# Moving the start addresses of matmul operands apart in an fp32 encoder layer

## The chip, the cores and the metric

The kernel runs on one core of a Trainium2 chip. The metric is the device time of one execution in microseconds (us). A core has TensorE (PE: matmuls, which read SBUF and write PSUM), VectorE (DVE), ScalarE (ACT), GpSimd (POOL) and SyncE (SP), which here issues the DMAs. SBUF has 128 partitions; a tile with 128 rows lies at one byte offset in all of them, and in this document an address is that offset.

## The reference

One layer of an encoder trunk over 256 rows of 2048 channels, all in fp32. With h = RMSNorm(x):

```python
proj = h @ w_in                                  # 2048 x 18464
yr = silu(rg) * groupnorm(retention(rope(rq), rope(rk), rv))
yg = silu(gz) * rmsnorm(gated_delta(l2(silu(conv(gq))), l2(silu(conv(gk))), silu(conv(gv)), g, beta))
x = x + (sigmoid(gate_a) * yr + sigmoid(gate_b) * yg) @ w_out
x = x + cross_attention(rms_norm(x), rms_norm(mem), w_xq, w_xkv) @ w_xo     # 4 heads, 256 memory rows
x = x + square(relu(rms_norm(x) @ w_ff1)) @ w_ff2                           # hidden 8192
return rms_norm(x)
```

Nearly all of the arithmetic is the product of 256 rows with weight matrices, some 390 MB of them, each read once.

## The kernel before, in words

**Splitting.** A matmul here takes its operands in the type float32r. So that the result has fp32 precision, each operand is split in two, hi (a copy in float32r, made by ScalarE) and lo (the remainder, made by VectorE), and a product is hi x hi + hi x lo + lo x hi, three passes.

**Weights.** `fetch` loads a block of 128 x 2048 elements into a tile `raw` (three buffers) on SyncE's queue. For each half of it, L89 writes `whi` (ScalarE) and L90 writes `wlo` (VectorE), tiles of 128 x 1024 with three buffers each.

**Activations.** They lie in *quads* (`new_quad`, name `q`): one tile of 128 x 4 x 512, that is, four feature blocks, each with 256 columns of hi and 256 of lo. Three pools hold quads: five shared ones (`quad_a`: the normalised input h1, the merged mixer output, the attention output, the MLP's hidden activations), four for the memory rows in the first stage (`memq`), and four of the tail (`quad_b`: the inputs of w_xq and of the MLP's first product).

**The two matmul loops.**
- `chunk` computes 256 rows x 512 columns of a product. The stationary operand is a 128 x 128 slice of a quad, the moving one 512 columns of whi or wlo (L130: hi x hi, L131: hi x lo, L132: lo x hi): 96 matmuls a call. There are 40 calls: 4 for the values of the attention (first stage, on `memq`), 4 for the retention's v, 16 for gates, 16 for the second MLP product. The last call holds the weights of its second half in buffers of `quad_b`, where they are the moving operand.
- `blocks` computes the transpose, 256 columns as two blocks of 128. The stationary operand is a 128 x 128 slice of whi or wlo, the moving one a row of a quad: L168 takes whi against hi and lo side by side (512 columns), L169 wlo against hi (256 columns). A call has 32 such pairs, and there are 96 calls with two blocks and one with one block (L481, 16 pairs): 24 for the delta rule, 8 for the retention's q and k, 8 for the attention's keys (on `memq`), 8 for w_out, 8 for w_xq, 8 for w_xo, 32 for the first MLP product. At its end L173 (ScalarE) and L174 (VectorE) add the two halves of the sum into a tile `bo` (two buffers of 128 x 256, shared by all calls), from which the caller goes on.

**The delta rule's norms.** In `gdn_stream`, for each of eight pairs of heads, three `blocks` calls give q, k and v; then L557 and L559 compute Gram matrices in PSUM, and four instructions on L563 multiply their diagonal blocks by the identity and add up the rows, which gives the squared norms. The products themselves go to a tile `dj` that nobody reads.

**Order.** The instructions of each engine are ordered by a scheduler that simulates a timeline from the program's order, priorities and the waits between instructions and buffers. Weight loads and splits have the highest priority, evacuations of PSUM the next. `blocks` and `chunk` write two PSUM banks a call, of which there are two sets.

**Where the tiles lie.** Tiles lie one behind another in the order of the pools, each rounded up to 32 bytes. raw has 8192 bytes a partition, whi and wlo 4096, a quad 8192, all multiples of 512. So raw, whi, wlo and the five shared quads, which follow each other, start at the same remainder modulo 512. Behind them come small tiles: a scratch row of 2048 bytes, two pairs of 32, two bo of 1024, four of 32. Adding up, the tail, and with it the quads of `quad_b`, start at 192 (modulo 512, counted from raw). The constants of the mixers (768 + 32 + 512 + 1024 + 1024 + 512 + 384 + 128 bytes) come where the tail later lies, and then `memq`, at 192 + 288 = 480, that is -32.

| tiles | start modulo 512, from raw | moving and stationary operand in a matmul lie apart by |
|---|---|---|
| whi, wlo (three each), five shared quads | 0 | 0 |
| `memq` | -32 | 32 |
| `quad_b` | 192 | 192 |

The slices that a matmul takes start at multiples of 512 bytes within their tile, so the distances hold for all of them.

Of the kernel before, what the change touches and what calls it, by code (L numbers as in the profile page):

```python
# [10 lines left out]
F32 = mybir.dt.float32  # L11
F32R = mybir.dt.float32r
# [5 lines left out]
P = 128  # L18
D = 2048
S = 256  # L20
# [8 lines left out]
C_GQ, C_GK, C_GV = 6144, 8192, 10240  # L29
C_GA, C_GZ, C_TA, C_TB = 12288, 12320, 14368, 16416  # L30
THETA = 10000.0
TWO_PI = 2.0 * math.pi
BIG = 1.0e30


def _short(v, bits):
    m, e = math.frexp(v)
    return math.ldexp(math.floor(m * (1 << bits)), e - bits)


PI_1 = _short(TWO_PI, 12)
PI_2 = _short(TWO_PI - PI_1, 11)
PI_3 = float(np.float32(TWO_PI - PI_1 - PI_2))
MAGIC = 1.5 * 2.0**23
# [3 lines left out]
def trunk(ctx: ExitStack, tc: tile.TileContext, x, mem, positions, norm_mix_g, w_in, conv_w, gdn_a_log, gdn_dt_bias,  # L48
# [7 lines left out]
    wp = ctx.enter_context(tc.tile_pool(name="wpipe", bufs=3))  # L56
    hqp = ctx.enter_context(tc.tile_pool(name="hq", bufs=1))
    sm = ctx.enter_context(tc.tile_pool(name="small", bufs=2))
# [8 lines left out]
    def bank():  # L67
        return psp.tile([P, 512], F32, name="b", tag="b", bufs=4)


    def fetch(pieces, k, n, rush=False, hold=None):

        raw = wp.tile([P, k * n], F32, name="raw", tag="raw", bufs=3)
        rv = raw.rearrange("p (k n) -> p k n", k=k)
        with tc.high_priority(offset=100000):
            for off, ap in pieces:
                src = ap.rearrange("(k p) n -> p k n", p=P)
                for ks in ((slice(0, k // 2), slice(k // 2, k)) if rush else (slice(0, k),)):
                    nc.sync.dma_start(rv[:, ks, off:off + ap.shape[1]], src[:, ks, :])
            got = []  # L80
            for i in range(2):
                if hold:
                    both = hold().both
                    hi, lo = (both[:, a:a + 2, :].rearrange("p a s -> p (a s)") for a in (0, 2))
                else:
                    hi = wp.tile([P, k * n // 2], F32R, name="whi", tag="whi", bufs=3)
                    lo = wp.tile([P, k * n // 2], F32R, name="wlo", tag="wlo", bufs=3)
                src = raw[:, i * k * n // 2:(i + 1) * k * n // 2]
                act.activation(hi, src, AF.Copy)  # L89
                vec.tensor_sub(lo, src, hi.bitcast(F32))  # L90
                got.append((hi.rearrange("p (k n) -> p k n", n=n), lo.rearrange("p (k n) -> p k n", n=n)))
        return got
# [12 lines left out]
        pass  # L105

    def new_quad(pl, bufs):
        both = pl.tile([P, 4, 2 * S], F32R, name="q", tag="q", bufs=bufs)
        quad = Quad((both[:, :, 0:S], both[:, :, S:2 * S]))
        quad.both = both  # L110
        return quad

    def quad_a():
        return new_quad(hqp, 5)

    def chunk(quads, pieces_of, evac, before=None, hold=None):
# [4 lines left out]
        if hold:  # L121
            parts[1:] = [(1, 0, 256, ps[1][:, :256]), (1, 256, 512, bank()[:, :256])]
        held = {q: fetch(pieces_of(q), 4, 512, hold=hold) for q in ((2, 3) if hold else ())}

        def products(q, i, part, halves):
# [8 lines left out]
        for q in range(4):  # L134
            if q not in held:
                if before:
                    before(q)
                halves = fetch(pieces_of(q), 4, 512, rush=before is not None and q == 0)
                for i in range(4):
                    for part in parts:  # L140
                        products(q, i, part, halves)
# [10 lines left out]
    def blocks(quads, w, c0, nb, evac):  # L152

        k = 16 // nb
        ps = stream_ps()
        n = nb * P
        for g in range(KT // k):
            halves = fetch([(0, w[g * k * P:(g + 1) * k * P, c0:c0 + n])], k, n)  # L160
            for i in range(k):
                kk = g * k + i
                xh, xhl = quads[kk // 4][0][:, kk % 4, :], quads[kk // 4].both[:, kk % 4, :]
                wh, wl = halves[i // (k // 2)]
                for b in range(nb):
                    bs = slice(b * P, (b + 1) * P)
                    lh, ll = wh[:, i % (k // 2), bs], wl[:, i % (k // 2), bs]
                    pe.matmul(ps[b], lh, xhl, start=kk == 0, stop=False)  # L168
                    pe.matmul(ps[b][:, :S], ll, xh, start=False, stop=kk == KT - 1)  # L169
        for b in range(nb):  # L170
            with tc.high_priority(offset=50000):
                o = sm.tile([P, S], F32, name="bo", tag="bo", bufs=2)
                act.activation(o, ps[b][:, S:], AF.Copy)  # L173
                vec.tensor_add(o, o, ps[b][:, :S])  # L174
                evac(b, o)
# [93 lines left out]
    kt_d = dram.tile([P, KT, S], F32, name="kt_d", tag="kt_d", bufs=1)  # L269
    vv_d = dram.tile([P, NT, D], F32, name="vv_d", tag="vv_d", bufs=1)  # L270
    memq = [new_quad(kv, 4) for _ in range(4)]
    ssqm = cp.tile([P, NT, 4], F32, name="ssqm")

# [32 lines left out]
    for k2 in range(8):  # L306
# [10 lines left out]
        for f in range(2):  # L317
            k = 2 * k2 + f
# [42 lines left out]
    def rounded(o, i, scale):  # L361
        vec.tensor_scalar(o, i, scale, MAGIC, op0=ALU.mult, op1=ALU.add)
        vec.tensor_scalar(o, o, -MAGIC, None, op0=ALU.add)

    def less(k, c):
        vec.scalar_tensor_tensor(av, k, -c, av, op0=ALU.mult, op1=ALU.add)

    rounded(hv, av, 1.0 / (4096.0 * TWO_PI))
    less(hv, 4096.0 * PI_1)
    vec.scalar_tensor_tensor(lv, hv, -4096.0 * PI_2, av, op0=ALU.mult, op1=ALU.add)  # L370
    rounded(lv, lv, 1.0 / TWO_PI)
    less(lv, PI_1)
# [131 lines left out]
    mx = mixer.enter_context(tc.tile_pool(name="mix", bufs=2))  # L504
# [14 lines left out]
    def gdn_stream(grp):  # L519
# [5 lines left out]
        for pr in range(2):  # L525
# [16 lines left out]
            for b in range(2):  # L542
                kh = mx.tile([P, 2, S], F32R, name="kh", tag="kh", bufs=2)
                kl = mx.tile([P, 2, S], F32R, name="kl", tag="kl", bufs=2)
                sq = mx.tile([P, S], F32, name="sq", tag="acc", bufs=2)
                act.activation(kh, kq[:, b], AF.Copy)
                vec.tensor_sub(kl, kq[:, b], kh.bitcast(F32))
                act.activation(sq, kq[:, b, 1], AF.Square)
                g0, g1 = bank(), bank()
                g0v = g0.rearrange("p (a n) -> p a n", a=2)  # L550
                g1v = g1[:, 0:256].rearrange("p (a n) -> p a n", a=2)
                if b == 0:
                    ssq = g1[:, 256:260].rearrange("p (b i) -> p b i", b=2)
                for t in range(NT):
                    pe.matmul(ssq[:, b, t:t + 1], sq[:, t * P:(t + 1) * P], ones[:, :1], start=True, stop=True)
                for n, (l, r) in enumerate(((kh, kh), (kh, kl), (kl, kh))):
                    pe.matmul(g0v, l[:, 0, 0:P], r, start=n == 0, stop=n == 2)  # L557
                for n, (l, r) in enumerate(((kh, kh), (kh, kl), (kl, kh))):
                    pe.matmul(g1v, l[:, 0, P:S], r[:, :, P:S], start=n == 0, stop=n == 2)  # L559
                grams.append((g0v, g1v))  # L560
                for t, src in enumerate((g0v[:, 0, 0:P], g1v[:, 0, :])):
                    dj = mx.tile([P, P], F32, name="dj", tag="dj", bufs=1)
                    vec.scalar_tensor_tensor(dj, src, 1.0, ident, op0=ALU.mult, op1=ALU.mult,  # L563
                                             accum_out=ssk[:, b, t:t + 1])
            ske = mx.tile([P, 2, NT], F32, name="ske", tag="ske", bufs=2)
# [214 lines left out]
    for j in range(5):  # L780
        if j < 4:
            group = gdn_stream(j)
        if prev is not None:
            if j < 4:
                quad = mx.tile([P, 4, S], F32, name="mg", tag="mg", bufs=3)
                kept.append(quad)
            else:
                quad = quad_a()
            gates(j - 1, prev[0], prev[1], quad, take_back if j == 4 else None)
        if j < 4:  # L790
            yr = mx.tile([P, NT, 512], F32, name="yr", tag="yr", bufs=1)
            yg = mx.tile([P, NT, 512], F32, name="yg", tag="yg", bufs=1)
            retention(j, yr)
            gdn_core(j, *group, yg)
            prev = (yr, yg)
# [9 lines left out]
    def quad_b():  # L805
        return new_quad(q2p, 4)
# [181 lines left out]
def _inv_freq():  # L988
    e = np.arange(0, RDK, 2, dtype=np.float32) / np.float32(RDK)
    return (np.float32(1.0) / np.power(np.float32(THETA), e)).astype(np.float32)  # L990

# [17 lines left out]
```

## Time and profile before

| | us |
|---|---|
| median of three runs (lowest, highest) | 2132.39 (2132.25, 2138.91) |
| the profiled execution | 2133.46 |
| its span, from the first to the last instruction | 2131.7 |
| TensorE busy | 2102.5 |
| VectorE busy | 1411.9 |
| ScalarE busy | 1092.3 |

In a row of instruction groups stand the line, the engine, the operation, output and inputs by the program's names, shapes and count, then busy time in us and the mean time of one in ns, then the idle time of the engine just before them and what ended it. Matmuls overlap each other in TensorE, so the mean of one is its latency; how fast they follow each other is seen from the starts in a timeline, or from a count in a stretch of time. PEld is TensorE's load of a stationary operand, which runs beside a matmul. PEclk is the clock that TensorE was granted, in tenths.

### The profile page before, as it was taken

The numbers are of one execution on the slowest core, as the hardware profiler recorded it, in microseconds if no ns is written. First come the engines' busy times: TensorE is split into PE (matmuls) and PEld (weight loads), VectorE is DVE, ScalarE is ACT, GpSimd is POOL, SyncE is SP. The second block draws the span as 40 slices with busy tenths as digits, with TensorE's granted clock in tenths as the row PEclk, the third lists the DMA queues.
The fourth block names the chain that finished last, engine by engine and source line by source line (L and its number), as shares of the span: only waits on it lengthen the run. The fifth ranks groups of instructions, "written<-read, shape, count | busy, mean of one in ns | idle before, by whom it ended". The sixth has DMA issues, their size and how long they took to land.

```text
span 2131.7 us, 28768 instructions
## 1 busy us (share of the span) xinstructions
PE 2102.5 (99%) x11172; PEld 1798.5 (84%) x11172; DVE 1411.9 (66%) x2225; ACT 1092.3 (51%) x1700; POOL 30.6 (1%) x39
## 2 busy tenths in 40 slices
PE   8999999899999999999999999999999999999998
PEld 6878888788888888888888888888888888888887
DVE  6756779588678866786567666666556545655655
ACT  7565565364555445645456555554434434434444
POOL 0000000000000000000000000000000000000000
PEclk9999999999999999999999999999999999999999
DMA  8777665455545654565457654566556556556653
GB/s 296 248 235 250 198 194 184 131 172 190 177 148 198 198 187 135 180 203 181 157 178 251 204 180 157 176 188 189 193 189 191 184 193 194 180 197 191 185 197 139
DMA packets 316009, 405.91 MB, mean 190 GB/s; under 512 B 16592, under 2 KB 224480, under 8 KB 315744
## 3 DMA queue, kind: packets, MB, share of 16 engines
q1 hardware_dynamic: 315872, 404.08, 58.6%
q8 instruction: 87, 1.43, 0.3%
q14 instruction: 50, 0.41, 0.1%
HBM read 390.40 MB, written 13.65 MB: 190 GB/s over the span
## 4 chain that ended last, share of the span: by engine, by line
PE 94%; DMA 2%; ACT 1%; DVE 1%; issue 0%; POOL 0%; SPq 0%; ACTq 0%; POOLq 0%; DVEq 0%
PE s L168 32%; PE s L169 16%; PE s L131 13%; PE s L130 13%; PE s L132 13%; PE b L646 2%; DMA dec_d<-dec_w 1%; ACT dec_w L471 1%; PE b L557 1%; PE b L100 0%; ACT whi L89 0%; DVE wlo L90 0%; PE b L102 0%; PE b L101 0%; PE b L215 0%
## 5 line engine op out<-in xcount | busy, mean ns | idle before, releaser
L90 DVE TENSOR_TENSOR wlo<-raw,whi 128x1024 fp32r<-128x1024 f32 x702 | 858.1, 1223 | 523.5 <-ACT whi L89 518.3
L89 ACT ACTIVATE whi<-raw 128x1024 fp32r<-128x1024 f32 x702 | 742.8, 1059 | 724.2 <-PE s L132 370.2
L168 PE MATMUL s<-q,whi 128*128 128x512 f32 x3088 | 1080.1, 397 | 0.3 <-DVE q L898 0.3
L169 PE MATMUL s<-q,wlo 128*128 128x256 f32 x3088 | 845.4, 281 | 6.4 <-DVE wlo L90 6.4
L168 PEld LDWEIGHTS s<-q,whi 128*128 128x128 f32 x3088 | 571.4, 188 | 125.2 <-DVE q L898 0.5
L169 PEld LDWEIGHTS s<-q,wlo 128*128 128x128 f32 x3088 | 580.1, 188 | 21.9 <-DVE wlo L90 10.2
L131 PE MATMUL s<-wlo,q 128*128 128x512 f32 x1264 | 495.3, 392 | 0.2 <-DVE wlo L90 0.2
L132 PE MATMUL s<-whi,q 128*128 128x512 f32 x1264 | 492.0, 390 | 0.0
L130 PE MATMUL s<-whi,q 128*128 128x512 f32 x1264 | 450.1, 391 | 0.0
L131 PEld LDWEIGHTS s<-wlo,q 128*128 128x128 f32 x1264 | 237.9, 188 | 49.8 <-DVE wlo L90 1.2
L130 PEld LDWEIGHTS s<-whi,q 128*128 128x128 f32 x1264 | 237.6, 188 | 50.1 <-ACT q L228 0.4
L132 PEld LDWEIGHTS s<-whi,q 128*128 128x128 f32 x1264 | 237.6, 188 | 48.8
L173 ACT ACTIVATE bo<-s 128x256 f32<-128x256 f32 x193 | 73.1, 379 | 121.6 <-PE s L169 121.6
L174 DVE TENSOR_TENSOR bo<-bo,s 128x256 f32<-128x256 f32 x193 | 80.4, 417 | 54.0 <-ACT bo L173 53.7
L512 DVE SCALAR_TENSOR_TENSOR acc<-bo,cw,acc 128x255 f32<-128x255 f32 (+2 forms) x144 | 67.1, 477 | 4.7 <-ACT acc L509 3.3
L612 DVE TENSOR_TENSOR pr<-lw,tw 32x31 f32<-32x31 f32 (+15 forms) x124 | 40.5, 326 | 9.1 <-DMA lw<-scr_l 6.9
L614 DVE TENSOR_TENSOR tw<-tw,pr 32x31 f32<-32x31 f32 (+15 forms) x124 | 40.7, 328 | 2.4
L747 ACT ACTIVATE gth<-s 128x512 f32<-128x512 f32 x32 | 18.9, 592 | 23.1 <-PE s L132 17.5
L937 DVE SCALAR_TENSOR_TENSOR res<-s,rstd3q,res 128x512 f32<-128x512 f32 (+1 forms) x32 | 22.3, 735 | 12.0 <-PE s L132 12.0
L509 ACT ACTIVATE acc<-bo,cw 128x256 f32<-128x256 f32 x48 | 24.2, 504 | 7.3 <-DVE bo L174 5.1
L926 DVE SCALAR_TENSOR_TENSOR hs<-bo 128x256 f32<-128x256 f32 x64 | 27.0, 422 | 1.1
L929 DVE TENSOR_TENSOR q<-hs,q 128x256 fp32r<-128x256 f32 x64 | 26.8, 418 | 0.9 <-ACT q L928 0.9
(292 smaller groups left out, 1086.7 us busy)
## 6 DMA issues: line engine op xcount, KB each, us to landing
raw<-w_in SPq DMA_DIRECT2D x144, 1024.0 KB
raw<-w_ff SPq DMA_DIRECT2D x128, 1024.0 KB
raw<-w_xkv SPq DMA_DIRECT2D x31, 1024.0 KB
raw<-w_out SPq DMA_DIRECT2D x16, 1024.0 KB
raw<-w_xq SPq DMA_DIRECT2D x16, 1024.0 KB
raw<-w_xo SPq DMA_DIRECT2D x16, 1024.0 KB
dec_d<-dec_w SPq DMA_DIRECT2D x16, 192.0 KB
dec<-dec_d SPq DMA_DIRECT2D x8, 384.0 KB
```

Of the source, the lines that this page charges most:

```text
L89: act.activation(hi, src, AF.Copy)
L90: vec.tensor_sub(lo, src, hi.bitcast(F32))
L130: pe.matmul(o, xh, wh, start=first, stop=False)
L131: pe.matmul(o, xh, wl, start=False, stop=False)
L132: pe.matmul(o, xl, wh, start=False, stop=last)
L168: pe.matmul(ps[b], lh, xhl, start=kk == 0, stop=False)
L169: pe.matmul(ps[b][:, :S], ll, xh, start=False, stop=kk == KT - 1)
L173: act.activation(o, ps[b][:, S:], AF.Copy)
L174: vec.tensor_add(o, o, ps[b][:, :S])
L512: vec.scalar_tensor_tensor(acc[:, d:], ps[:, :S - d], cw[:, j, blk:blk + 1], acc[:, d:], op0=ALU.mult, op1=ALU.add)
L614: vec.tensor_sub(tw[:, j + 1:32, 0:j + 1], tw[:, j + 1:32, 0:j + 1], pv)
L646: pe.matmul(pv[:, i, :], lhs(i), rhs[:, i, :], start=True, stop=True)
```

## The change

Each tile of a quad gets 8 more elements at its end (32 bytes), and each whi and wlo 40 more (160 bytes). Nothing is read or written there; the extra elements only move what lies behind them. The tile `dj` (512 bytes) is given up: L563 now writes the first half of a tile from the two buffers of `bo`. The instructions and their sizes are the same.

```diff
+STAGGER_Q, STAGGER_W = 8, 40
...
-                    hi = wp.tile([P, k * n // 2], F32R, name="whi", tag="whi", bufs=3)
-                    lo = wp.tile([P, k * n // 2], F32R, name="wlo", tag="wlo", bufs=3)
+                    hi, lo = (wp.tile([P, k * n // 2 + STAGGER_W], F32R, name=nm, tag=nm, bufs=3)[:, :k * n // 2]
+                              for nm in ("whi", "wlo"))
...
     def new_quad(pl, bufs):
-        both = pl.tile([P, 4, 2 * S], F32R, name="q", tag="q", bufs=bufs)
+        both = pl.tile([P, 8 * S + STAGGER_Q], F32R, name="q", tag="q", bufs=bufs)
+        both = both[:, :8 * S].rearrange("p (f s) -> p f s", f=4)
...
                 for t, src in enumerate((g0v[:, 0, 0:P], g1v[:, 0, :])):
-                    dj = mx.tile([P, P], F32, name="dj", tag="dj", bufs=1)
+                    dj = sm.tile([P, S], F32, name="dj", tag="bo", bufs=2)[:, :P]
                     vec.scalar_tensor_tensor(dj, src, 1.0, ident, op0=ALU.mult, op1=ALU.mult,
                                              accum_out=ssk[:, b, t:t + 1])
```

By the same sums, the starts modulo 512 counted from raw become: whi 0, 160, 320; wlo -32, 128, 288; the shared quads -64, -32, 0, 32, 64; `memq` 64, 96, 128, 160; `quad_b` 288, 320, 352, 384. Buffers are used in rotation, so over a call a moving operand meets stationary operands at many distances.

## The prediction

> **What bounds the kernel now.** I read the page first, from the busy shares down to the costliest groups.
>
> ```profile
> span 2131.7 us, 28768 instructions
> PE 2102.5 (99%) x11172; PEld 1798.5 (84%) x11172; DVE 1411.9 (66%) x2225; ACT 1092.3 (51%) x1700; POOL 30.6 (1%) x39
> ...
> PEclk9999999999999999999999999999999999999999
> ...
> PE 94%; DMA 2%; ACT 1%; DVE 1%; issue 0%; POOL 0%; SPq 0%; ACTq 0%; POOLq 0%; DVEq 0%
> ...
> L168 PE MATMUL s<-q,whi 128*128 128x512 f32 x3088 | 1080.1, 397 | 0.3 <-DVE q L898 0.3
> L169 PE MATMUL s<-q,wlo 128*128 128x256 f32 x3088 | 845.4, 281 | 6.4 <-DVE wlo L90 6.4
> ...
> L131 PE MATMUL s<-wlo,q 128*128 128x512 f32 x1264 | 495.3, 392 | 0.2 <-DVE wlo L90 0.2
> ...
> L132 PE MATMUL s<-whi,q 128*128 128x512 f32 x1264 | 492.0, 390 | 0.0
> L130 PE MATMUL s<-whi,q 128*128 128x512 f32 x1264 | 450.1, 391 | 0.0
> ```
>
> TensorE is busy for 99% of the span, at full granted clock, and 94% of the chain of waits is TensorE. The view of waits, for TensorE alone, says how little it waits; its longest row is
>
> ```profile
> PE s L169 <- DVE wlo L90: 6.4, 8, 1.5
> ```
>
> So the time is a count of matmuls times the spacing between their starts. The 390 ns in the group rows is the latency of one, not the spacing, since they overlap. Almost everything is two loops: `chunk` (L130 to L132, 3 x 1264 = 3792 matmuls of 512 columns; moving operand whi or wlo, stationary operand a slice of a quad q) and `blocks` (3088 pairs L168 + L169; moving operand q, stationary whi or wlo). Whatever the change does must show in those spacings, and a nanosecond on each of the 3792 is 3.8 us. So I looked for stretches in which the same instruction runs with operands at different addresses. First the view of windows: stretch, its length, busy time and count of each engine, clock, DMA share, GB/s.
>
> ```profile
> core 0: us, PE busy (x) PEld busy (x) DVE busy (x) ACT busy (x) POOL busy (x), PEclk, DMA share, GB/s
> 30.00:50.00 20.00, 20.00 (x87) 15.82 (x86) 12.29 (x23) 15.36 (x26) 0.00 (x0) 1.00 0.86 303
> 1120.00:1200.00 80.00, 80.00 (x460) 69.74 (x460) 58.95 (x91) 46.88 (x75) 0.00 (x0) 1.00 0.76 237
> 1505.00:1585.00 80.00, 80.00 (x354) 66.25 (x353) 41.79 (x40) 31.68 (x33) 0.00 (x0) 1.00 0.59 197
> 1600.00:1670.00 70.00, 70.00 (x399) 60.82 (x398) 43.74 (x61) 33.09 (x50) 0.00 (x0) 1.00 0.61 185
> 2112.80:2115.40 2.60, 2.60 (x13) 2.07 (x12) 0.00 (x0) 0.00 (x0) 0.00 (x0) 1.00 0.00 0
> ```
>
> Then the groups of 30 to 50 us and, of 1120 to 1200 us, the three groups in it:
>
> ```profile
> L132 PE MATMUL s<-whi,q 128*128 128x512 f32 x29 | 11.4, 394 | 0.0
> L131 PE MATMUL s<-wlo,q 128*128 128x512 f32 x28 | 11.2, 399 | 0.0
> L130 PE MATMUL s<-whi,q 128*128 128x512 f32 x29 | 10.3, 395 | 0.0
> L201 PE MATMUL b<-ident,grow 48*128 48x48 f32 x1 | 0.3, 258 | 0.0
> ```
>
> ```profile
> L168 PE MATMUL s<-q,whi 128*128 128x512 f32 x227 | 79.0, 397 | 0.0
> L169 PE MATMUL s<-q,wlo 128*128 128x256 f32 x227 | 61.8, 279 | 0.0
> L215 PE MATMUL b<-ident,yg 128*128 128x128 f32 x6 | 0.8, 272 | 0.0
> ```
>
> And from the timeline, the first and the last of twelve starts near the end of the run, where `chunk` works on weights held in the second set of quads:
>
> ```profile
> 2112.82 0.40 PE L131 MATMUL s<-q 128*128 128x512 f32 x1
> 2113.05 0.39 PE L132 MATMUL s<-q 128*128 128x512 f32 x1
> ...
> 2115.38 0.39 PE L130 MATMUL s<-q 128*128 128x512 f32 x1
> ```
>
> A window counts an instruction that overlaps its edge, so I divide by one fewer. `chunk` in the MLP (1505 to 1585 us): 80 / 353 = 226.6 ns. `chunk` in the first stage (30 to 50 us): about 19.9 / 85 = 234 ns. `chunk` on the held weights: 2.56 / 11 = 232.7 ns, with VectorE, ScalarE and DMA at nothing. `blocks` in the output projection (1120 to 1200 us), with about 0.7 us taken off for the six transposes: 79.3 / 226 = 351 ns a pair. `blocks` in the MLP (1600 to 1670 us): 70 / 198.5 = 352.6 ns a pair.
>
> Why should the same matmul take 226.6 in one place and 233 in another? Load on the other engines and DMA doesn't order them: the emptiest stretch is among the slow ones. Distance does. By adding up tile sizes (the section on the kernel has the table), in the MLP's `chunk` moving and stationary operand begin at the same place modulo 512 bytes; in the first stage they are 32 bytes apart, and on the held weights 192. My reading: while a matmul streams its moving operand, TensorE loads the next stationary one, and the two readers disturb each other least when their start addresses are equal modulo 512.
>
> **The change, part by part.** *`chunk` on the five shared quads.* Of 40 calls, 4 (first stage) use other quads, and the last holds 24 matmuls of 512 columns on held weights: 3792 - 4 x 96 - 24 = 3384 matmuls stand at distance zero now. After the change three whi, three wlo and five quads begin at eleven starts, at 0, 160, 320; -32, 128, 288; -64, -32, 0, 32, 64 (modulo 512, from raw's start). Of the 30 combinations of a weight buffer and a quad, two are still at zero (whi 0 with q 0, wlo -32 with q -32). The price of a distance that isn't zero is 234 - 226.6 = 7.4 ns by the one row and 232.7 - 226.6 = 6.1 by the other; I take 6.7, the middle, as the new distances lie around both. 3384 x 28/30 x 6.7 = +21.2 us. Bounds: only the two distances that I have seen (32 and 192, four of the 30) cost anything: 3384 x 4/30 x 6.7 = +3.0; all at the dearer price: 3384 x 28/30 x 7.4 = +23.4. I take the upper part, since both distances seen cost nearly the same though they are far apart.
>
> The Trainium skill ("TensorE: Matmul & The Clock Gate", Part 2, step by step) says that TensorE has two independent read ports and that "Loading the next tile's weights doesn't steal SBUF read bandwidth from the running matmul." By that rule this term is nothing, and the sum 23 us less. The rows at 226.6 and 232.7 ns, of one instruction at one clock, don't bear it out.
>
> *`chunk` in the first stage.* 384 matmuls go from a distance of 32 everywhere to 24 combinations with two at zero: 384 x 2/24 x 6.7 = -0.2 us. The held weights: no combination at zero before or after, 0.
>
> *`blocks`.* With a quad of the shared five (24 + 8 calls in the mixers, 8 + 8 in the two output projections, one short call of 16 pairs: 48 x 32 + 16 = 1552 pairs) the distance is zero now and the pair takes 351; with the second set (w_xq and the MLP, 40 x 32 = 1280 pairs) it is 192, and 352.6. So zero buys only 1.6 ns here: 1552 x 28/30 x 1.6 = +2.3, and back 1280 x 2/24 x 1.6 = -0.2. But a distance can also be luckier in `blocks`; in the k projection, where q is 32 bytes below the weights, some stretches run like this:
>
> ```profile
> 153.86 0.39 PE L168 MATMUL s<-q,whi 128*128 128x512 f32 x1
> ...
> 155.60 0.39 PE L168 MATMUL s<-q,whi 128*128 128x512 f32 x1
> ```
>
> These are five pairs in 1.74 us, 348 ns each. Bounds: all pairs to 348 is 1552 x -3.1 + 1280 x -4.6 = -10.7 us; all to 355, as far above the MLP's row as this lies below it, is +9. I take +2, as the long rows stand close together.
>
> *dj goes into bo's two buffers.* 32 small VectorE instructions, the same in number and length. But dj now stands in line with bo. The timeline around the first of eight such places:
>
> ```profile
> 258.86 0.42 DVE L174 TENSOR_TENSOR bo<-bo,s 128x256 f32<-128x256 f32 x1 [0.69 <-ACT bo L173]
> 259.38 0.51 ACT L509 ACTIVATE acc<-bo,cw 128x256 f32<-128x256 f32 x1 [0.55 <-DVE bo L174]
> ...
> 260.66 0.29 DVE L563 SCALAR_TENSOR_TENSOR dj<-b,ident 128x128 f32<-128x128 f32 x1
> 260.87 0.08 DVE L563 DVE_READ_ACCUMULATOR dj<-b,ident 128x1 f32 x1
> 261.27 0.28 DVE L563 SCALAR_TENSOR_TENSOR dj<-b,ident 128x128 f32<-128x128 f32 x1
> ```
>
> The next call's bo (written by ScalarE just before 258.86) comes after the four dj in the program, and shares a buffer with the third, so it can start only when that ends, near 260.95: about 2.5 us late. Behind it on ScalarE wait L509 and the next whi, and behind that TensorE. Its s banks are double, and a `blocks` call takes 32 x 351 ns = 11.2 us, so a bank that is read 2.5 us late is still free in time; and the schedule is made with this wait in view. I take 0. With the cover gone: 8 x 2.5 = +20 us; a changed order can also win back some of the waits, the longest of which is the 6.4 us above.
>
> *ScalarE, VectorE, DMA.* Same instructions, sizes and transfers. Their waits on TensorE lengthen with it; nothing else depends on them. 0.
>
> **Sum.** 21.2 - 0.2 + 2.1 + 0 = +23.1 us. The profiled execution took 2133.46 us (span 2131.7 and 1.8 around it), which is 1.1 above the median 2132.39; 2133.5 + 23.1 = 2156.6, against the median 2155.5. I predict 2155.
>
> **The rivals.**
> - *Faster.* The new distances avoid the disturbance instead of adding it: nothing shows `chunk` at 64, 96, 128, 160 or 256. Then `chunk` stays at 226.6, its lowest long row, and `blocks` falls to 348 throughout: 2132.4 - 10.7 = 2122. It decides only while `chunk` rises by less than 10.7 / 3384, 3.2 ns; both distances seen are above 6. By the skill's same page (back-to-back issue gap, about 216 ns for 512 columns, warm) a `chunk` free of all disturbance would give 3384 x 10.6, some 36 us on top; no row of a long stretch here comes near it. Chance 0.09.
> - *The change does nothing* (the rule of the ports, or the first stage's 234 has another cause): 2132. Against it stand the twelve starts with every other engine idle. 0.06.
> - *Half of it.* The pattern repeats at a shorter distance than 512, or only some distances cost. With a period of 128, seven of 30 combinations are at zero: 3384 x 23/30 x 6.7 = 17.4; if only a third cost, 7.6. So 2139 to 2150. 0.15.
> - *dj's wait reaches TensorE* on top of the rest: 2175. 0.03.
> - *As forecast*, 2147 to 2167: 0.67.
>
> **How the numbers follow.** A measurement of this kernel tells 0.3%, 6.4 us, from no change. Faster: 0.09. Same: 0.06 and a small part of "half of it", together 0.08. Slower: 0.83. The range leaves out the faster case, no change, and the doubled wait (0.18): from 2137, below the low end of "half of it", to 2168, which is the sum with `chunk` at 7.4 and `blocks` at +9 (2132.4 + 23.2 + 9 = 2165) and a little for a changed order.
>
> **What would show it.** In the window of the MLP's first `chunk` stretch the count over 80 us falls from 354 to about 344, with ScalarE and VectorE no busier. The three `chunk` stretches of the MLP lengthen by some 2.4 us each (384 x 6.3 ns). Window counts of `blocks` stay within 1%. TensorE's waits stay near 20 us in all; a new row of ScalarE's bo waiting on dj would show the shared buffer, and a longer wait of TensorE for wlo that it matters. The prediction is wrong if `chunk` stays at 226 to 228 (then the place modulo 512 isn't what I read), or if `blocks` moves by 10 ns or more a pair, in either direction, since 3088 of them outweigh the rest.

## The result, and the profile after

The changed kernel takes 2156.18 us (median of four runs, 2154.55 to 2162.98); the kernel before, measured beside it, 2135.53. The ratio is 1.0103, with a 95% interval of 1.0072 to 1.0133: slower by about 1%. The forecast was 2155, slower. The profiled execution took 2155.71 us. The page of the changed kernel (its lines stand two or three further down):

```profile
span 2154.0 us, 28778 instructions
PE 2120.8 (98%) x11172; PEld 1802.8 (84%) x11172; DVE 1411.6 (66%) x2225; ACT 1091.4 (51%) x1700; POOL 29.7 (1%) x39
...
PE 92%; DMA 3%; DVE 1%; ACT 1%; SPq 1%; issue 0%; POOL 0%; ACTq 0%; POOLq 0%; DVEq 0%
...
L171 PE MATMUL s<-q,whi 128*128 128x512 f32 x3088 | 1081.1, 396 | 2.0 <-DVE bo L177 0.9
L172 PE MATMUL s<-q,wlo 128*128 128x256 f32 x3088 | 848.5, 282 | 5.4 <-DVE wlo L92 5.3
...
L134 PE MATMUL s<-wlo,q 128*128 128x512 f32 x1264 | 499.2, 395 | 0.6 <-DVE wlo L92 0.6
```

Each engine has as many instructions as before, VectorE and ScalarE are as busy as before (1411.6 and 1091.4 us), and TensorE is busy for 18 us more. But it also fell from 94% to 92% of the chain: there is some waiting that was not there. Three windows show this, first in the kernel before, then in the changed one: the stretch around the first delta core (380 to 440 us), 80 us of `chunk` in the MLP, 80 us of `blocks` in the MLP. The columns are the stretch, its length, TensorE's busy time and count, clock, DMA share, GB/s.

```profile
380.00:440.00 60.00, 52.57 (x318) 1.00 0.35 112
1506.00:1586.00 80.00, 80.00 (x355) 1.00 0.58 193
1594.00:1674.00 80.00, 80.00 (x455) 1.00 0.62 191
```

```profile
380.00:440.00 60.00, 48.90 (x287) 0.94 0.30 98
1523.00:1603.00 80.00, 80.00 (x347) 1.00 0.58 191
1613.00:1693.00 80.00, 80.00 (x458) 1.00 0.62 188
```

In 80 us of `chunk` there are 347 matmuls in place of 355: the spacing went up. `blocks` in the MLP is a little denser, not sparser (458 against 455). And in the stretch from 380 us TensorE does 31 matmuls fewer in the same 60 us, with its clock down to 0.94.

Summing the distance from each matmul's start to the next over all matmuls of the trace gives a ledger of the span; the last two columns are experiments told below (us):

| | before | after | extra bytes alone | dj in bo alone |
|---|---|---|---|---|
| `chunk`, 3792 matmuls of 512 columns | 870.0 | 886.3 | 886.2 | 869.3 |
| `blocks`, 3088 pairs | 1097.9 | 1101.1 | 1095.3 | 1104.0 |
| all other matmuls | 161.2 | 164.2 | 162.8 | 172.3 |
| ahead of the first matmul | 2.6 | 2.5 | 2.5 | 2.4 |
| span | 2131.7 | 2154.0 | 2146.8 | 2148.0 |

So 16.3 of the 22.3 us are `chunk`, and the other 6 lie in `blocks` and in the small matmuls, where the prediction had 2.

### The profile page after: what moved, and what is told of

Its sections match the earlier page's. It is cut to its first block, busy times and chain, and to the rows that moved or that the text cites. A ratio compares the mean times of both kernels' runs of the same rounds, so it can differ in the third digit from the quotient of the medians.

```text
span 2154.0 us, 28778 instructions
## 1 busy us (share of the span) xinstructions
PE 2120.8 (98%) x11172; PEld 1802.8 (84%) x11172; DVE 1411.6 (66%) x2225; ACT 1091.4 (51%) x1700; POOL 29.7 (1%) x39
## 4 chain that ended last, share of the span: by engine, by line
PE 92%; DMA 3%; DVE 1%; ACT 1%; SPq 1%; issue 0%; POOL 0%; ACTq 0%; POOLq 0%; DVEq 0%
PE s L171 31%; PE s L172 16%; PE s L135 13%; PE s L134 13%; PE s L133 13%; PE b L649 2%; DMA dec_d<-dec_w 1%; DMA row<-crow 1%; DVE wlo L92 1%; DMA xc<-x 1%; ACT dec_w L474 0%; PE b L560 0%; PE b L102 0%; DMA ct<-scr_t 0%; PE b L104 0%
## 5 line engine op out<-in xcount | busy, mean ns | idle before, releaser
L171 PE MATMUL s<-q,whi 128*128 128x512 f32 x3088 | 1081.1, 396 | 2.0 <-DVE bo L177 0.9
L171 PEld LDWEIGHTS s<-q,whi 128*128 128x128 f32 x3088 | 573.5, 189 | 125.3 <-ACT whi L91 2.0
L135 PE MATMUL s<-whi,q 128*128 128x512 f32 x1264 | 498.1, 395 | 0.0
L133 PE MATMUL s<-whi,q 128*128 128x512 f32 x1264 | 455.7, 395 | 0.0
L940 DVE SCALAR_TENSOR_TENSOR res<-s,rstd3q,res 128x512 f32<-128x512 f32 (+1 forms) x32 | 22.3, 736 | 12.1 <-PE s L135 12.1
L931 ACT ACTIVATE q<-hs 128x256 fp32r<-128x256 f32 x64 | 26.2, 410 | 0.0
```

The lines of the kernel that those rows point to most:

```text
L133: pe.matmul(o, xh, wh, start=first, stop=False)
L135: pe.matmul(o, xl, wh, start=False, stop=last)
```

## The experiments

### Which half of the change costs what

The first experiment takes all extra bytes out again and leaves dj in bo's buffers. Its instructions stand in the order of the changed kernel.

```diff
-STAGGER_Q, STAGGER_W = 8, 40
+STAGGER_Q, STAGGER_W = 0, 0
```

> All extra bytes are taken out again (both constants 0), and only dj stays in bo's buffers; the order of the instructions is that of the changed kernel. If the distance between moving and stationary operand sets the spacing: chunk back at 226 to 227 ns a matmul (354 matmuls in 80 us of the MLP), and the time within 0.3% of before, with at most 8 us more from the waits that the profile of the changed kernel has over that of before. If dj and the new order are the cause: 2150 us or more, and chunk stays near 232 ns.

Measured: 2149.21 us, ratio 1.0064 (1.0047 to 1.0081). Both theories were half right, which means that there are two causes. Its windows, the same three stretches, and three more within the first:

```profile
380.00:440.00 60.00, 47.26 (x240) 0.77 0.23 68
1523.00:1603.00 80.00, 80.00 (x355) 1.00 0.57 191
1610.00:1690.00 80.00, 80.00 (x455) 1.00 0.63 191
```

```profile
405.00:410.00 5.00, 3.54 (x15) 0.50 0.00 0
410.00:415.00 5.00, 3.47 (x15) 0.50 0.00 0
415.00:420.00 5.00, 4.22 (x20) 0.50 0.00 0
```

`chunk` is back at 355, so distance has nothing to do with this part. The whole loss lies around the first delta core: 78 matmuls fewer in 60 us than before, and the clock at half from 405 to 420 us.

The second experiment is the counterpart: all extra bytes, but dj in a tile of its own (in bf16, to take less room). Every engine's instructions stand in the order of the kernel before.

```diff
-                    dj = sm.tile([P, S], F32, name="dj", tag="bo", bufs=2)[:, :P]
+                    dj = mx.tile([P, P], mybir.dt.bfloat16, name="dj", tag="dj", bufs=1)
```

> All the extra bytes of the change, but dj keeps a tile of its own (in bf16, so that it fits); the instructions stand in the order of the kernel before. If the distances cost what the spacings of the changed kernel say (chunk 232 ns against 227.6 over 3792 matmuls, 16 us; blocks 1 to 2 us the other way): +14 to +17 us, 2148 to 2152 us, with the clock undisturbed. If dj in bo's buffers makes most of the loss: 2141 us or less.

Measured: 2151.75 us, ratio 1.0081 (1.0062 to 1.0101), and its windows:

```profile
380.00:440.00 60.00, 52.83 (x309) 0.97 0.32 98
1516.00:1596.00 80.00, 80.00 (x347) 1.00 0.57 190
1605.00:1685.00 80.00, 80.00 (x459) 1.00 0.63 192
```

As forecast: `chunk` at 347 in 80 us without any help from dj, TensorE as busy around the first delta core as before (52.83 us), +15.1 us in the ledger. Only the clock was not quite undisturbed, at 0.97 in that stretch. The two halves together would make 1.45%; the whole change makes 1.03%. They don't add up, and the ledger says where: dj costs 16.3 us of span in the one profile and 7.2 in the other (2154.0 - 2146.8), though all instructions stand in the same order in both.

The windows of 380 to 440 us give an estimate of the parts. TensorE's idle time there grew from 7.4 us (60 - 52.57) to 11.1 in the changed kernel, which is 3.7 more, and the clock of 0.94 takes 6% of 60 us, 3.6: together 7.3 of the 7.2. With dj alone it is 5.3 us more idle time and at most 13.8 by the clock of 0.77 (at most, since TensorE's waits lie partly in the same time), against 16.3. By this estimate much of what dj costs is the clock, and how long it stays down differs from execution to execution: of the four of the first experiment, the one with a mean clock of 0.997 took 2144.63 us, and the one with 0.992 took 2152.09.

### What it is about dj

Two more kernels without extra bytes. In one, bo has three buffers:

```diff
-                    dj = sm.tile([P, S], F32, name="dj", tag="bo", bufs=2)[:, :P]
+                    dj = sm.tile([P, S], F32, name="dj", tag="bo", bufs=3)[:, :P]
...
-                o = sm.tile([P, S], F32, name="bo", tag="bo", bufs=2)
+                o = sm.tile([P, S], F32, name="bo", tag="bo", bufs=3)
```

> No extra bytes, dj in bo's buffers, but three of these in place of two. If the loss with dj alone comes from waiting for one of two buffers: 2133 to 2138 us, and TensorE is not left idle around 390 to 430 us. If sharing as such, by another order of the instructions, is the cause: 2144 us or more.

Measured: 2144.77 us, ratio 1.0048 (1.0029 to 1.0066). The third buffer wins back some 4 us at most, and the two intervals overlap. In the other kernel, dj shares the scratch row of the sums of squares:

```diff
-                    dj = sm.tile([P, S], F32, name="dj", tag="bo", bufs=2)[:, :P]
+                    dj = sm.tile([P, 512], F32, name="dj", tag="junk", bufs=1)[:, :P]
```

> No extra bytes; dj shares the one scratch row that the sums of squares write, in place of bo's buffers. If it is the turn-taking with bo that reorders the work ahead of the first delta core: the core starts near 401 us again as before, the clock stays up, 2133 to 2139 us. If any shared buffer for dj costs the same: 2144 us or more.

Measured: 2134.87 us, ratio 1.0003 (0.9993 to 1.0013): the loss is gone. So sharing a buffer isn't what costs, for this one is the only one of its kind; taking turns with bo is. The view of waits for ScalarE has the new wait by name, 12.2 us over six times in the changed kernel, 12.6 with dj alone and 8.4 with three buffers:

```profile
ACT bo L176 <- DVE dj L566: 12.2, 6, 3.3
```

```profile
ACT bo L176 <- DVE dj L566: 12.6, 6, 3.3
```

```profile
ACT bo L176 <- DVE dj L566: 8.4, 5, 2.6
```

ScalarE waits there, but TensorE's own wait for bo is small: the row of L171 on the page of the changed kernel, shown at the top, has 0.9 us on it. What changed for TensorE is the order. The groups of 380 to 403 us, first in the kernel before, then with three buffers:

```profile
L168 PE MATMUL s<-q,whi 128*128 128x512 f32 x62 | 21.4, 395 | 0.0
L169 PE MATMUL s<-q,wlo 128*128 128x256 f32 x62 | 16.7, 279 | 0.0
```

```profile
L171 PE MATMUL s<-q,whi 128*128 128x512 f32 x38 | 13.1, 395 | 0.0
L172 PE MATMUL s<-q,wlo 128*128 128x256 f32 x40 | 10.6, 278 | 0.0
L642 PE MATMUL b<-alt,t 128*128 128x128 f32 x16 | 2.1, 281 | 1.3 <-DVE t L632 1.3
```

Before, 62 pairs of `blocks` ran in that time, and the delta core's first matmuls (L639 there) began at 400.7 us. Where dj stands in line with bo, the scheduler puts some two dozen pairs behind the core; it then begins at 393.8 to 394.7 us, waits for its operands (the row of L642), and runs its chain of small matmuls and evacuations with less work ahead of it. When the scratch row is shared, the core begins at 402.2 us. That it is this order and not the wait itself is my reading of these rows; no run has the one without the other, and none has the order with the clock held up.

### What it is about the distance

Three theories were left for `chunk`: only the distance between moving and stationary operand counts; or its changing from one matmul to the next; or the weights' or quads' own places. First the quads alone get their bytes, then the weights alone (dj in bo in both):

```diff
-STAGGER_Q, STAGGER_W = 8, 40
+STAGGER_Q, STAGGER_W = 8, 0
```

> Only the quads get their 32 bytes; whi and wlo stay at 0, the shared quads stand at 0, 32, 64, 96, 128. So over the 24 or 48 matmuls that one quad serves the distance is constant. If a distance that isn't zero costs by itself: four of five quads are dear, chunk near 232 ns, 2150 us or more. If what costs is the change of distance from one matmul to the next, while a constant distance lets TensorE settle: chunk near 227 to 228 ns, 2132 to 2142 us.

```diff
-STAGGER_Q, STAGGER_W = 8, 40
+STAGGER_Q, STAGGER_W = 0, 40
```

> Only whi and wlo get their 160 bytes; dj in bo's buffers; the quads all at -64. No combination of a weight buffer and a shared quad is at zero. If distance decides: chunk in the MLP near 233 ns (344 matmuls in 80 us), 2150 to 2165 us. If it is the quads' spread that costs: chunk at 227 ns.

Measured: 2158.2 us, ratio 1.0111 (1.0096 to 1.0126), and 2153.89 us in one run. From the starts of the first MLP `chunk` call to the last of that stretch, a matmul takes 232.1 and 231.9 ns (before 226.8, after 231.8). Either half of the stagger costs `chunk` as much as both. And with the quads alone the distance is constant for as long as one quad serves: sorted by it, in all `chunk` calls, the matmuls on the quad at zero run at 228 ns and those on the quads at 32, 64, 96 and 128 at 232 to 234. A constant distance that isn't zero is no help; it is the distance itself.

But a distance of zero helps only where it stays. In the kernel before, most groups of twelve matmuls on one half of a weight block run at 226.6 ns a matmul. In the changed kernel the lowest mean of such a group, over the 280 on the shared quads, is 230.4, although 4 of the 15 combinations of a pair of weight buffers (a whi with its wlo) and a quad have a moving operand at zero (modulo 256, the period found below). So in a sequence of changing distances the matmuls at zero don't get the price of zero; why is open.

Then one distance for all five shared quads, in the kernel before, with dj and order left alone and the tiles behind at their old places (modulo 512); N is 8, 16, 32 and 64 elements of four bytes:

```diff
-
+    quad_0 = [[vec.memset(hqp.tile([P, N], F32, name="pad_a", tag="pad_a", bufs=1), 0.0), new_quad(hqp, 5), vec.memset(hqp.tile([P, 128 - N], F32, name="pad_b", tag="pad_b", bufs=1), 0.0)][1]]
     def quad_a():
-        return new_quad(hqp, 5)
+        return quad_0.pop() if quad_0 else new_quad(hqp, 5)
```

> The kernel before with 32 bytes ahead of the five shared quads and 480 behind them: one distance, 32, for all of them, the rest where it was (dj has its own tile; two small memsets more). If a distance that isn't zero costs by itself, as in the first stage of the kernel before: chunk 233 to 234 ns, about 2155 us. If a constant distance is as good as zero: 226.6 ns, 2132 us.

> One distance, 64, between the weights and all shared quads, order as before. By the quads at 64 in the run with quads alone moved (chunk near 230 ns): 2138 to 2146 us. If every distance but zero costs alike: chunk 233 ns, 2149 us.

> The same at 128, half of the 256 at which the spacing came back. By the quads at 128 in the run with quads alone moved: chunk 232 to 233 ns, about 2148 us. If the pattern repeats at 128: 226.7 ns, 2134 us.

> The same with 256 bytes ahead of the shared quads and 256 behind: one distance, half of 512. If only the place modulo 512 counts and zero is best: chunk 233 ns, about 2155 us. If the pattern repeats at 256 or a shorter distance, or a constant distance is as good as zero: 226.6 ns, 2132 us.

Measured, with the spacing of `chunk` in the first MLP stretch and the mean of a pair of `blocks` on the shared quads without its waits:

| quads ahead of weights by, bytes | us | ratio | `chunk`, ns | `blocks`, ns a pair |
|---|---|---|---|---|
| 0 (before) | 2135.0 | | 226.8 | 349.8 |
| 32 | 2151.33 | 1.0079 (1.0063 to 1.0094) | 233.3 | 347.7 |
| 64 | 2157.26 (one run) | | 233.3 | 351.4 |
| 128 | 2150.63 (one run) | | 232.4 | 350.5 |
| 256 | 2134.12 | 0.9995 (0.9985 to 1.0004) | 226.8 | 349.7 |

The last column moves by up to about half a nanosecond with how the waits are left out; the differences within it stay the same to 0.2 ns. The windows of 80 us of MLP `chunk` at 32, 128 and 256 bytes:

```profile
1514.00:1594.00 80.00, 80.00 (x344) 1.00 0.57 190
```

```profile
1515.00:1595.00 80.00, 80.00 (x345) 1.00 0.57 192
```

```profile
1507.00:1587.00 80.00, 80.00 (x355) 1.00 0.58 192
```

At 256 bytes the spacing is that of zero, to a tenth of a nanosecond: of the distances tried, what counts is the distance modulo 256, not 512. In between all distances tried are dear, by 5.6 to 6.5 ns. Nothing but the quads' place differs between the four padded kernels. The expectation of 230 ns at 64 was wrong: in the run with quads alone, the quad 64 ahead ran at nearly 234 too.

### A kernel from the findings

`blocks` likes 32 bytes ahead (347.7 against 352.8 ns in the tail, where the distance is 192), `chunk` likes zero. The first stage stands at 32 for `chunk`, the tail at 192 for `blocks`. Two pads, and nothing else; the tail then stands at 192 + 96 = 288, which is 32 modulo 256:

```diff
-    memq = [new_quad(kv, 4) for _ in range(4)]
+    vec.memset(kv.tile([P, 8], F32, name="pad", tag="pad", bufs=1), 0.0); memq = [new_quad(kv, 4) for _ in range(4)]
...
-    q2p = ctx.enter_context(tc.tile_pool(name="q2", bufs=1))
+    q2p = ctx.enter_context(tc.tile_pool(name="q2", bufs=1)); vec.memset(q2p.tile([P, 24], F32, name="pad", tag="pad", bufs=1), 0.0)
```

> The kernel before with 32 bytes ahead of the four quads of the first stage (distance 0 in place of 32) and 96 ahead of the four quads of the tail (distance 32 in place of 192, the quad ahead of the weights, at which blocks ran 347.7 ns a pair in the run with 32 bytes). If distance decides: chunk in the first stage 227 in place of 234 ns (384 matmuls, -2.6 us), blocks in the MLP and w_xq 347.7 in place of 352.8 ns a pair (1280 pairs, -6.5 us), together 2124 to 2127 us. If only zero is good and all other distances are alike: at most -3 us, 2132.

Measured over five rounds: 2126.72 us, ratio 0.9959 (0.9944 to 0.9973). It is faster than both kernels, and the time lies in the range forecast, though the interval reaches a third of the gain to either side. Its windows in the first stage, in the MLP's `chunk` and in its `blocks`:

```profile
30.00:50.00 20.00, 20.00 (x89) 1.00 0.92 315
```

```profile
1504.00:1584.00 80.00, 80.00 (x355) 1.00 0.58 191
1592.00:1672.00 80.00, 80.00 (x462) 1.00 0.62 189
```

89 matmuls in the first stage's 20 us in place of 87, `chunk` in the MLP unchanged, and 462 in 80 us of `blocks` in place of 455: 347 ns a pair. So the distance sets the spacing of the first stage too, and it is worth something in both directions.

Only one of the two pads shortened the kernel, though. By the same sums as in the ledger, `blocks` went from 1097.9 to 1091.1 us, which is 6.8 of the 6.7 us that the span lost, and `chunk` stayed where it was, to 0.2 us. The four `chunk` calls of the first stage last 98.4 us together, counted from the first to the last start of each, where they lasted 98.5: the closer spacing is taken back by pauses between the matmuls. DMA is busy for 0.92 of the stretch in the window above, so it is likely that the weights come no sooner, which no run shows. The 2.6 us forecast for this stage did not come.

## Why the prediction was right, and where not

The total was right, 2155 against 2156.18, with a forecast of +23.1 us of span against +22.3. The main step, that leaving distance zero makes `chunk` slower, was right and is shown. The parts of the sum were less so: two terms were some 5 us too high each, and dj's, at 0, some 7 too low. That they cancelled is luck.

- *`chunk` on the shared quads*, forecast +21.2 us, measured +16.3 for all of `chunk`. The mechanism was right: distance, not load, sets the spacing, and zero is the best of those tried (256 is as good). The price in the sum was too high. At one constant distance it is 5.6 to 6.5 ns, about as taken (6.7), but in the changed kernel's mixture it is 5.0 (231.8 - 226.8). The period is 256 and not the 512 of the prediction, so four of 30 combinations stand at zero and not two. That doesn't explain the difference: the sum would still give 19.1 (3384 x 26/30 x 6.5), and the combinations at zero don't run at 226.8 ns in the mixture (no group of twelve matmuls under 230.4). So what was mis-sized is the step that counts each combination at the price it has when the distance stays the same; how a mixture adds up is open.
- *Two readers that disturb each other* was offered as the reason. The runs show the effect of the distance between moving and stationary operands; they don't show what happens inside, nor whether it is the next stationary operand or the present one that counts, since both lie at the same distance in the runs with one distance.
- *`blocks`*, forecast +2.1, measured -2.6 us with the extra bytes alone. The bounds of -10.7 and +9 held it. The taken value rested on 0 and 192 alone, and gave the tail only -0.2. In the trace with the extra bytes alone the 1280 pairs of the tail, leaving 192, take 2.2 ns less each, some 2.8 us, and the pairs on the shared quads little more than before.
- *First stage and held weights*: small as forecast.
- *dj in bo's buffers* was the step that failed, though the total doesn't show it. It stood at 0, because "a bank that is read 2.5 us late is still free in time; and the schedule is made with this wait in view". The wait came, 12.2 us in all, and the bank was nearly in time (0.9 us). But the schedule that has the wait in view is another schedule: it moved some two dozen pairs from before the delta core to behind it, and TensorE idled more there and lost its clock for a while. That cost 7.2 us in the whole change and 14 us alone, where the prediction's price with the cover gone was 20. Had I put it at 7, the sum would have been 8 us too high: 5 by the `chunk` term and 5 by `blocks`, less 1.6 that the other matmuls took.
- *The rivals.* "The change does nothing" fell with the first `chunk` window. The rule of the Trainium skill ("TensorE: Matmul & The Clock Gate", Part 2) that loading weights doesn't take bandwidth from the running matmul would make this term nothing, and the runs don't bear that out for these operands: the kernels with 256 and 32 bytes, at 226.8 and 233.3 ns, differ by nothing but the quads' place. Whether it is bandwidth that is lost, they don't show. "Faster" would have needed `chunk` to rise by less than 3.2 ns; it rose by 5.0. "Half of it" had the shorter period right and the size wrong. "dj's wait reaches TensorE" came true for about a third of its 20 us (7.2), though as idle time and a lower clock around the delta core, with 0.9 us of waiting for bo.
- *What was to show it.* The window's count was to fall to about 344 and fell to 347; the MLP's three `chunk` stretches were to lengthen by 2.4 us each and did so by 2.0 (86.8 to 88.8 us from first to last start); the row of bo waiting on dj appeared, and its note, that only TensorE's longer wait for wlo would make it matter, was wrong: that wait shrank from 6.4 to 5.3 us.

## What to carry to other kernels

Where TensorE is busy all the time, measure the spacing of its matmuls in several stretches: one instruction at two spacings is a lead, and the starts of its operands are worth adding up before anything else. Here equal starts modulo 256 bytes, the same from one matmul to the next, were best for a stream of 512 columns whose stationary operand changes each time, so spreading buffers "so that they differ" was a loss. Setting the tail's tiles to a better distance was a gain of 0.4%; in the first stage the same closer spacing gained nothing, so ask of each stretch whether something else holds it up. And a scratch output put into a busy rotation isn't free because its instruction is short: it takes turns with the others there, and the scheduler answers with another order, whose cost here lay around the first delta core, where TensorE had the least other work.

## What the runs showed of the hardware that I had not expected

The distance between the starts of moving and stationary operands changes the spacing of float32r matmuls with 512 columns: 226.8 ns at 0 and 256 bytes, 233.3 at 32 and 64, 232.4 at 128, all with VectorE, ScalarE and DMA busy, and 232.7 at 192 with all three idle. For pairs of 512 and 256 columns the best of the distances tried is another one (347.7 ns at 32, 349.8 at 0, 352.8 at 192).

With dj alone, TensorE's clock was at half from 405 to 420 us, around the delta core, although TensorE was busy for about 3.5 of every 5 us there or more. Its longest wait of the whole stretch of 380 to 440 us is this one, which ends at 393.8 us:

```profile
PE b L642 <- DVE t L632: 3.2, 1, 3.2
```

The Trainium skill ("TensorE: Matmul & The Clock Gate", Part 1) puts the fall to half down to a window of about 3.4 us of idleness, and in one kernel to frequent short idle times between groups of matmuls. Here no wait was as long as that window, and after 394 us none was over 1.5 us.

In the profile of the kernel before, the same chain of small matmuls, some 23 us long, kept its full clock, although TensorE was busy for less of it (2.75, 3.46 and 2.77 us in the three stretches of 5 us from 405 to 420 us). So how busy TensorE is doesn't tell by itself whether the clock falls, and what does is open. Nor is the fall dj's alone: three executions of the kernel before with a mean clock of 0.995 took 2139.57 to 2141.61 us, where those at 0.998 and 0.999 took 2131.35 to 2136.54.
